# Stores of sixteen heads, V loads behind Q and K: a change to the transfer order of tree attention

## The chip, the cores and the metric

The kernel runs on one core of one Trainium2 chip. The metric is the device time of one execution in microseconds; a time of the kernel is the median of several runs. The 16 transfer (DMA) engines of the core move all data between memory and SBUF. GpSimd (POOL), SyncE (SP) and ScalarE (ACT) issue transfers; loads that turn float32 into bf16 go through GpSimd's queue.

## The reference, cut to what matters

```python
# Q, K, V: (8, 12, 512, 64) float32; 96 heads of 512 x 64
mask = np.zeros((seq, seq))          # node i sees itself and its ancestors in a binary tree
for i in range(seq):
    mask[i, i] = 1
    parent = i
    while parent > 0:
        parent = (parent - 1) // 2
        mask[i, parent] = 1
scores = np.einsum('bhqd,bhkd->bhqk', Q, K) * scale + (1 - mask) * (-1e9)
weights = softmax(scores)            # over the keys
out = np.einsum('bhqk,bhkd->bhqd', weights, V)
```

## The kernel before, in words

Row 4p+t of a head lies on partition p, slot t. A step handles a pair of heads, so there are 48 steps. In step i TensorE makes the scores of pair i (L458, L466, L491, L501), the product with V of pair i - 1 (L551), and in turn the transposes of K (odd steps, L401) or Q (even steps, L433) for two pairs some steps ahead: from step 9 on, step i transposes K of pairs i + 3 and i + 4 in odd steps, Q of pairs i + 2 and i + 3 in even steps. Pairs interlace from pair 8 on, two pairs for four heads, so K and Q of heads 72 to 75 are needed in steps 33 and 34. ScalarE takes the exponentials (L472, L476, L507). VectorE takes reciprocal and product that normalise a pair and write the output tile (L581, L583, in float32), moves transposes out of PSUM (L412 to L420, L441) and makes part of the V copies.

The product with V writes one PSUM tile, `ob`, of which there is one copy; the product of the next pair waits until VectorE has normalised the pair before.

V comes in six tiles of sixteen heads (`vst`, three buffers), each in three transfers: the upper 64 rows, and the even and the odd of the others. It is then copied ("spread") into the layout of the mask, into `vt` (two buffers of three tiles). From tile 4 on, VectorE makes copy "M" of tile o + 1 in two halves of eight heads, at the end of steps 8o and 8o + 2, and copy "Y" at the end of steps 8o + 4 and 8o + 6 (`STEADY_VECTOR`, L695). "M" reads all 128 partitions, so it needs all three transfers of the tile. GpSimd makes the rest: four "top" copies, "X", "Z0" and "Z1" (`spread_top`, `spread_pool`). Copy M of tile 5 (heads 80 to 95) is due in steps 32 and 34, the product with its first heads in step 41.

GpSimd works off a list written out by hand (`pool_program`, L606), in order: loads of K and Q of up to eight heads (1 MB of memory each for eight heads), V in three parts (1, 0.5 and 0.5 MB), its copies, and stores (1 MB for eight heads). `pool(i)` hands out the list as far as `ready` allows; that fixes only the program's order, since the chip's engines wait by semaphores. In the built program a transfer of GpSimd waits besides for the landing of its transfer eight places earlier. Up to head 63 the list is explicit; from head 64 on a loop writes it (L628 to L642): K and Q of eight heads, V parts 32 heads ahead, copies, and a store of eight heads as soon as the heads loaded are `BEHIND` = 56 ahead of it.

Output tiles hold eight heads (`VO`, `NOUT` = 11 buffers). Heads 76 to 79 are stored by SyncE, in four transfers of 64, 27, 25 and 12 rows (`store_apart`, after step 41). Heads 88 to 95 are stored by SyncE and ScalarE two or one at a time as they are ready.

The mask enters the scores through a matrix of codes (L186): 40 rows, loaded by SyncE and copied by ScalarE to partitions 64 and up (L209).

Of the kernel before, what the change touches and what calls it, by code (L numbers as in the profile page):

```python
# [9 lines left out]

CODE = 2048.0
CODE_ROWS = 40
NOUT = 11
BEHIND = 56

# [44 lines left out]
def _nodes(u0, units=UNITS, parity=False):  # L62
    return np.concatenate([4 * _rows(kind, parity) + t for kind, t in units[u0:u0 + 4]])


def _path(n):

    return [1.0 if c == "1" else -1.0 for c in bin(n + 1)[3:]]


def _mask_codes():

    k1 = np.zeros((64, 128), np.float32)
    q1 = np.zeros((64, 4, 128), np.float32)
    k2 = np.zeros((64, 128), np.float32)
    q2 = np.zeros((64, 4, 128), np.float32)  # L80
    k1w = np.zeros((64, 128), np.float32)
    k2w = np.zeros((64, 128), np.float32)

    def key(codes, row, bits, col, node):
        path = _path(node)
        assert len(path) <= bits
        codes[row:row + len(path), col] = np.array(path) * CODE
        codes[row + bits, col] = -len(path) * CODE

    def query(codes, row, bits, col, node):  # L90
        path = _path(node)[:bits]
        codes[(slice(row, row + len(path)),) + col] = path
        codes[(row + bits,) + col] = 1.0

    for c, node in enumerate(_nodes(TOP)):
        key(k1, 0, 7, c, node)
    for c, node in enumerate(_nodes(TOP, WUNITS)):
        key(k1w, 0, 7, c, node)
    for t in range(4):
        for c, node in enumerate(_nodes(TILE2[t])):  # L100
            key(k2, 10 * t, 9, c, node)
        for c, node in enumerate(_nodes(WTILE2[t], WUNITS, True)):
            key(k2w, 10 * t, 9, c, node)
        for p in range(128):
            node = 4 * p + t
            query(q1, 0, 7, (PLACE[t], p), node)
            if p >= 32:
                query(q2, 10 * (SELF[t] if p < 64 else t), 9, (PLACE[t], p), node)
    return np.concatenate([k1, q1.reshape(64, -1), k2, q2.reshape(64, -1), k1w, k2w], axis=1)
# [10 lines left out]
def kernel(  # L120
# [7 lines left out]
    nc = tc.nc  # L128
    B, H, S, D = Q.shape
    P = nc.NUM_PARTITIONS  # L130
    assert S == 512 and D == 64 and P == 128 and (B * H) % 4 == 0
    scale = float(1.0 / np.sqrt(D))
    NH = B * H
    NQ = NH // 4
    NP = 2 * NQ
    WIDE = 8
    KB, VB, VO = 8, 16, 8
    assert NH % VB == 0

    fp32 = mybir.dt.float32  # L140
# [12 lines left out]

    perm_dram = nc.inline_tensor(_eye_twice().astype(ml_dtypes.bfloat16), name="tree_eye")
    code_dram = nc.inline_tensor(
        _mask_codes()[0:CODE_ROWS].astype(ml_dtypes.bfloat16), name="tree_codes"
    )

    ctx.enter_context(tc.manual_schedule())
# [6 lines left out]
    small = ctx.enter_context(tc.tile_pool(name="small", bufs=4))  # L166
    opool = ctx.enter_context(tc.tile_pool(name="opool", bufs=NOUT))
    psS = ctx.enter_context(tc.tile_pool(name="psS", bufs=1, space=bass.MemoryType.PSUM))
# [4 lines left out]
    codes = consts.tile([P, 1536], bf16)  # L173
# [4 lines left out]
    def first_load(eng, name, src):  # L178
        eng.dma_start(
            out=first[name][:, :, :, :].rearrange("p h t d -> p h (t d)"), in_=src[:, 0:2, :]  # L180
        )
# [1 line left out]
    first_load(nc.sync, "K", Kr)  # L183
    nc.scalar.dma_start(out=ptile[:, :], in_=perm_dram.ap())
    first_load(nc.scalar, "Q", Qr)
    nc.sync.dma_start(out=codes[0:CODE_ROWS, :], in_=code_dram.ap())  # L186
    eye = ptile[:, 0:256]

    def eye_blocks(first, x, y):
# [74 lines left out]
    def head(i, a):  # L264

        return 2 * i + a if i < WIDE else 4 * (i // 2) + i % 2 + 2 * a
# [178 lines left out]
    def turn(name, i):  # L445
        heads = [head(i + b, a) for b in range(2 if i >= WIDE else 1) for a in range(2)]
        assert all((name, h) in issued for h in heads), (name, i)
        {"kst": (narrow_k, wide_k), "qst": (narrow_q, wide_q)}[name][i >= WIDE](i)
        return i + (2 if i >= WIDE else 1)
# [140 lines left out]
    def store(eng, h0, n, step=1, p0=0, p1=P):  # L590
        g, f = divmod(h0, VO)
        return eng.dma_start(  # L592
            out=Or[p0:p1, h0:h0 + step * (n - 1) + 1:step, :],
            in_=ofs[g][p0:p1, f:f + step * (n - 1) + 1:step, :, :].rearrange(
                "p h t d -> p h (t d)"
            ),
        )

    APART, APART_AT, APART_ROWS = 76, 41, (0, 64, 91, 116, P)

    def store_apart():

        for p0, p1 in zip(APART_ROWS, APART_ROWS[1:]):
            store(nc.sync, APART, 4, 1, p0, p1)

    def pool_program():  # L606

        ops = [
            (load_k, 2, 2), (load_q, 2, 2), (load_v, 0, 4), (load_v, 4, 4),
            (load_k, 4, 2), (load_k, 6, 2), (load_q, 4, 2), (load_k, 8, 4),  # L610
            (load_q, 6, 2), (load_q, 8, 4), (load_v, 8, 8), (load_k, 12, 4),
            (load_q, 12, 4), (load_k, 16, 4), (load_rows, 1, "upper"),
            (load_q, 16, 4), (load_rows, 1, "even"), (load_k, 20, 4), (load_rows, 1, "odd"),
            (load_q, 20, 4), (load_k, 24, 8), (load_q, 24, 4), (load_rows, 2, "upper"),
            (load_q, 28, 4), (load_k, 32, 4), (load_rows, 2, "even", "odd"),
            (load_q, 32, 8), (load_k, 36, 4), (load_rows, 3, "upper"),
            (spread_pool, (1, "Z0", 8, 16), (1, "Z1", 8, 16)),
            (load_k, 40, 8), (load_q, 40, 8), (load_rows, 3, "even", "odd"),
            (spread_top, 2, 0, 16), (spread_pool, (2, "Z0", 0, 16), (2, "Z1", 0, 16)),
            (load_q, 48, 4), (spread_pool, (2, "X", 0, 8)),  # L620
            (load_k, 48, 8), (spread_pool, (2, "X", 8, 16)),
            (load_q, 52, 4), (load_rows, 4, "upper"), (spread_top, 3, 0, 16),
            (load_k, 56, 8), (load_q, 56, 8), (load_rows, 4, "even", "odd"),
            (spread_pool, (3, "X", 0, 8), (3, "Z0", 0, 16), (3, "Z1", 0, 16), (3, "X", 8, 16)),
            (load_rows, 5, "upper"), (store, nc.gpsimd, 0, VO),
        ]
        loaded, stored = 88, 1
        for h in range(64, NH, KB):  # L628
            top = [(spread_top, h // VB + 0)] if h % VB == 8 and 4 <= h // VB + 0 < NH // VB else []
            ops += [(load_k, h, KB)] + top + [(load_q, h, KB)]  # L630
            while loaded < min(h + 32, NH):
                names = ("even", "odd") if loaded % VB else ("upper",)
                ops.append((load_rows, loaded // VB) + names)
                loaded += KB
            if top:
                o = h // VB
                ops.append((spread_pool, (o, "X", 0, 16), (o, "Z0", 0, 16), (o, "Z1", 0, 16)))
            while VO * stored + VO + BEHIND <= h + KB:
                ops.append((store, nc.gpsimd, VO * stored, VO))
                stored += 1  # L640
        for g in range(stored, NH // VO - 1):
            ops.append((store, nc.gpsimd, VO * g, APART - VO * g if g == APART // VO else VO))  # L642
        return ops

    def ready(op, i):
# [62 lines left out]
    def pool(i):  # L708
        while program and ready(program[0], i):
            op = program.pop(0)  # L710
            op[0](*op[1:])
# [18 lines left out]
    for i in range(NP + 1):  # L730
        steps = FIRST[i] if i < len(FIRST) else "SVK" if i % 2 else "SVQ"
        for step in steps:
            if step == "S" and i < NP:
                scores1(i)
                scores2(i)
            if step == "V" and i >= 1:
                values(i - 1)
                norm(i - 1)
                valued = True
            if step == "K" and kdone < NP:  # L740
                kdone = turn("kst", kdone)
            if step == "Q" and qdone < NP:
                qdone = turn("qst", qdone)
            if step == "W":
                nc.scalar.copy(
                    out=codes[64:64 + CODE_ROWS, 1280:1536], in_=codes[0:CODE_ROWS, 1280:1536]
                )
            if step == "X":
                spin("s1" if valued else "ob", 2)
            if step == "D":  # L750
                spread_by(nc.vector.tensor_copy, BY_VECTOR, STEADY_VECTOR, i)
            if step == "A":
                spread_by(nc.scalar.copy, BY_SCALAR, {}, i)
        if "D" not in steps:
            spread_by(nc.vector.tensor_copy, BY_VECTOR, STEADY_VECTOR, i)
        if "A" not in steps:
            spread_by(nc.scalar.copy, BY_SCALAR, {}, i)
        pool(i)
        if i == APART_AT:
            store_apart()  # L760
        if i >= NP - 3 and i < NP:
            store(nc.sync, head(i - 1, 0), 2, 2)
    assert not program
# [32 lines left out]
```

## Time and profile before

| | |
|---|---|
| median of 3 runs | 135.01 us (134.32 to 135.81) |
| profiled execution, its own time | 134.27 us |
| span of the profiled execution | 132.4 us, clock 0.97 |
| PE busy | 113.4 us (86%) |
| VectorE busy | 100.1 us (76%) |
| ScalarE busy | 94.4 us (71%) |
| GpSimd busy | 72.9 us (55%) |
| memory read, written | 37.94 MB, 12.58 MB |

The span runs from the first to the last instruction; the execution's own time is 1.87 us longer. The page cuts the span into 40 slices of 3.31 us and gives busy shares in tenths. Its chain of waits goes back from the last instruction to whatever released it. A row of the timeline gives start, duration, engine, line and operation, output and input, and in brackets how long the engine was idle before it and what ended that. PE is TensorE, DVE is VectorE, ACT is ScalarE, POOL is GpSimd, SP is SyncE. `kst`, `qst` and `vst` are the loaded K, Q and V; `of` is the output tile; `kq` holds transposed K or Q; `e` the exponentials; `s` and `ob` are PSUM tiles.

### The profile page before, as it was taken

To read this page: it belongs to the slowest core of one execution; us is meant where nothing else is said; L and a number is where in the kernel's file an instruction comes from. 1 tells how busy PE (TensorE), PEld (TensorE's weight loads), DVE (VectorE), ACT (ScalarE), POOL (GpSimd) and SP (SyncE) were. 2 spreads that over 40 slices of the span, in tenths; PEclk is the share of its full clock that TensorE was granted. 3 is DMA by queue.
4 is the path that set the end of the run, shared out by engine and by line. 5 is a ranking of instruction groups with operands and counts; after the bars stand their busy time and mean duration, and the time that the engine had idled before them with its cause. 6 is when DMAs were issued, how large, how long until landed. Compare 5 with 4: busy or idle time off the path is not lost.

```text
span 132.4 us, 5523 instructions
## 1 busy us (share of the span) xinstructions
PE 113.4 (86%) x2414; PEld 79.0 (60%) x2417; DVE 100.1 (76%) x249; ACT 94.4 (71%) x153; POOL 72.9 (55%) x100
## 2 busy tenths in 40 slices
PE   6886979999999899899989299999999997989800
PEld 2343755766676677676766276767666774756500
DVE  3539779889999999987965668899978896674620
ACT  4369577988888788778768455889796975969600
POOL 6999625454375999987732799437289600002000
PEclk9999999999999999999999958999999999999985
DMA  3999999999999999999999999999999999999992
GB/s 109 237 184 193 199 196 201 202 202 205 199 202 201 203 203 207 200 210 197 205 204 197 298 273 202 266 300 226 341 214 330 244 279 399 401 399 401 395 351 72
DMA packets 32244, 32.26 MB, mean 244 GB/s; under 512 B 1204, under 2 KB 29492, under 8 KB 32220
## 3 DMA queue, kind: packets, MB, share of 16 engines
q0 software_dynamic: 29824, 29.63, 114.7%
q1 hardware_dynamic: 1836, 1.83, 4.0%
q10 hardware_dynamic: 560, 0.46, 1.1%
q8 instruction: 19, 0.31, 0.9%
q14 instruction: 5, 0.04, 0.1%
HBM read 37.94 MB, written 12.58 MB: 382 GB/s over the span
## 4 chain that ended last, share of the span: by engine, by line
DMA 57%; PE 26%; POOL 5%; issue 4%; ACT 2%; DVE 1%; ACTq 0%; POOLq 0%
DMA vst<-in_V_dram 38%; DMA qst<-in_Q_dram 13%; PE ob L551 8%; DMA kst<-in_K_dram 7%; PE s L458 4%; PE s L466 3%; PE qtp L433 3%; PE ktp L401 2%; PE s L491 2%; PE s L501 2%; POOL vt L336 2%; POOL kst L251 1%; PE s L551 1%; ACT e L472 1%; ACT e L507 1%
## 5 line engine op out<-in xcount | busy, mean ns | idle before, releaser
L476 ACT ACTIVATE e<-s 128x1024 bf16<-128x1024 f32 x40 | 40.9, 1023 | 21.5 <-PE s L466 20.8
L551 PE MATMUL ob<-vt,e 128*128 128x65 bf16 (+1 forms) x940 | 38.0, 198 | 5.2 <-DVE of L583 3.8
L551 PEld LDWEIGHTS <-e 128*128 128x128 bf16 (+1 forms) x960 | 30.6, 103 | 13.7 <-DVE of L583 4.0
L507 ACT ACTIVATE e<-s 128x384 bf16<-128x384 f32 x80 | 34.7, 491 | 0.0
L583 DVE TENSOR_TENSOR of<-ob,rec 128x512 f32<-128x512 f32 x47 | 32.5, 691 | 1.6
L336 POOL COPY vt<-vst 32x512 int32<-32x512 int32 (+1 forms) x32 | 24.1, 754 | 7.2 <-DVE vt L336 3.9
L336 DVE COPY vt<-vst 64x1024 bf16<-64x1024 bf16 (+6 forms) x42 | 17.6, 420 | 5.7 <-DMA vst<-in_V_dram 5.1
L458 PE MATMUL s<-codes 40*128 40x512 bf16 x96 | 19.6, 395 | 1.2 <-issue 0.4
L581 DVE RECIPROCAL rec<-ob 128x8 f32<-128x8 f32 x47 | 9.7, 205 | 13.3 <-PE ob L551 12.7
L466 PE MATMUL s<-kq 64*128 64x512 bf16 x96 | 18.8, 382 | 0.0
L592 POOL DMA_DIRECT2D out_dram<-of x11 | 9.8, 895 | 15.5 <-DVE of L583 13.4
L280 POOL DMA_DIRECT2D vst<-in_V_dram x15 | 10.8, 723 | 12.7 <-DMA vst<-in_V_dram 7.0
L501 PEld LDWEIGHTS <-kq 64*128 64x128 bf16 x320 | 12.6, 95 | 4.7 <-issue 0.4
L501 PE MATMUL s<-kq 64*128 64x160 bf16 (+1 forms) x320 | 15.1, 210 | 0.0
L491 PE MATMUL s<-codes 40*128 40x384 bf16 x80 | 14.1, 339 | 0.1
L401 PE MATMUL ktp<-ptile,kst 128*64 128x128 bf16 x320 | 12.9, 224 | 1.2 <-issue 0.9
L441 DVE COPY kq<-qtp 128x1024 bf16<-128x1024 bf16 x20 | 13.6, 682 | 0.2 <-PE qtp L433 0.2
L433 PE MATMUL qtp<-ptile,qst 128*64 128x128 bf16 x320 | 12.7, 219 | 0.8 <-issue 0.7
L251 POOL DMA_DIRECT2D qst<-in_Q_dram x13 | 9.6, 738 | 5.1 <-DMA kst<-in_K_dram 1.7
L251 POOL DMA_DIRECT2D kst<-in_K_dram x12 | 9.1, 756 | 5.6 <-PE s L466 1.6
L491 PEld LDWEIGHTS <-codes 40*128 40x128 bf16 x80 | 6.4, 95 | 8.8 <-issue 1.1
L472 ACT ACTIVATE e<-s 128x1024 bf16<-128x1024 f32 x8 | 8.2, 1022 | 4.9 <-PE s L466 4.8
(42 smaller groups left out, 120.2 us busy)
## 6 DMA issues: line engine op xcount, KB each, us to landing
out_dram<-of POOLq DMA_DIRECT2D x10, 1024.0 KB, 16.3
kst<-in_K_dram POOLq DMA_DIRECT2D x8, 512.0 KB, 15.3
qst<-in_Q_dram POOLq DMA_DIRECT2D x7, 512.0 KB, 16.8
vst<-in_V_dram POOLq DMA_DIRECT2D x12, 256.0 KB, 14.1
vst<-in_V_dram POOLq DMA_DIRECT2D x6, 512.0 KB, 13.4
qst<-in_Q_dram POOLq DMA_DIRECT2D x8, 256.0 KB, 11.7
kst<-in_K_dram POOLq DMA_DIRECT2D x6, 256.0 KB, 11.7
out_dram<-of SPq DMA_DIRECT2D x4, 256.0 KB, 7.3
```

Of the source, the lines that this page charges most:

```text
L251: return nc.gpsimd.dma_start(out=kept[b][:, h0 % KB:h0 % KB + n, :, :].rearrange("p (g x) t d -> p g (x t d)", x=2), in_=wide[:, h0 // 2:( ...
L336: return copy(out=dst, in_=src)
L401: nc.tensor.transpose(out=columns(kp[64 * a:64 * a + 64, :], mixed, (256, 2), (leaves - mixed, 2), (1, 32)), in_=st[:, 2 * i % KB // 2 + a ...
L433: nc.tensor.transpose(out=halves[64 * a:64 * a + 64, :, c:c + 64], in_=st[:, 2 * i % KB // 2 + a, 4 * u + t, :], identity=ptile[:, 0:128],)
L458: nc.tensor.matmul(out=sp[:, a, :], lhsT=(k1code if i < WIDE else k1wide)[64 * a:64 * a + CODE_ROWS, :], rhs=(q1code[64 * a:64 * a + CODE_ ...
L466: nc.tensor.matmul(out=sp[:, a, :], lhsT=keys(i, a, TOP), rhs=qTs[i][64 * a:64 * a + 64, :, :].rearrange("p t c -> p (t c)"), start=False, ...
L476: ) if i < WIDE else nc.scalar.activation(
L491: nc.tensor.matmul(out=flat[:, a, :, :].rearrange("p u (t c) -> p u t c", t=4)[:, :, :, 16:64], lhsT=k2wide[64 * a:64 * a + CODE_ROWS, :], ...
L501: nc.tensor.matmul(out=flat[:, a, :, lo:hi], lhsT=keys(i, a, WTILE2[t]), rhs=qT[64 * a:64 * a + 64, :, lo:hi], start=False, stop=t == 1, s ...
L507: nc.scalar.activation(out=e2s[i % NE][:, a, :, 32:128].rearrange("p t (r u) -> p t r u", u=2), in_=flat[:, a, :, :].rearrange("p u (t r) ...
L551: nc.tensor.matmul(out=ob[lo:hi, a, 65 * t:65 * t + 65], lhsT=e[:, a, PLACE[t], lo:hi], rhs=vt[vtile[tile_v][0]][:, head(i, a) % VB, vtile ...
L583: nc.vector.tensor_tensor(out=ofs[g][:, first:last + 1:step, :, :], in0=o4[:, a:a + n, :, 0:D], in1=rec[:, a:a + n, :, :].to_broadcast([P, ...
```

## The change

Output tiles hold sixteen heads and there are six of them. GpSimd's list is written out to its end. From head 64 on its order is: K64, Q64, store 0 to 15; K72, the top copies of V tile 4, Q72, Z0 and Z1; V tile 5 upper, X of tile 4, V tile 5 even and odd; K80, Q80, store 16 to 23; K88, Q88; stores 24 to 31 and 32 to 47; top, Z0 and Z1 of tile 5; store 48 to 63; X of tile 5; stores 64 to 71, 72 to 79, 80 to 87. `store_apart` goes, and with it the four transfers of SyncE. Q of heads 48 to 55 is one load and not two. The codes are loaded with 48 rows, of which 40 are used as before. The tables of VectorE's and ScalarE's copies stay.

```diff
-NOUT = 11
-BEHIND = 56
+NOUT = 6
+LOAD_ROWS = 48
...
-    KB, VB, VO = 8, 16, 8
+    KB, VB, VO = 8, 16, 16
...
-        _mask_codes()[0:CODE_ROWS].astype(ml_dtypes.bfloat16), name="tree_codes"
+        _mask_codes()[0:LOAD_ROWS].astype(ml_dtypes.bfloat16), name="tree_codes"
...
-    nc.sync.dma_start(out=codes[0:CODE_ROWS, :], in_=code_dram.ap())
+    nc.sync.dma_start(out=codes[0:LOAD_ROWS, :], in_=code_dram.ap())
...
-    APART, APART_AT, APART_ROWS = 76, 41, (0, 64, 91, 116, P)
-
-    def store_apart():
-
-        for p0, p1 in zip(APART_ROWS, APART_ROWS[1:]):
-            store(nc.sync, APART, 4, 1, p0, p1)
...
-            (load_q, 48, 4), (spread_pool, (2, "X", 0, 8)),
+            (load_q, 48, 8), (spread_pool, (2, "X", 0, 8)),
             (load_k, 48, 8), (spread_pool, (2, "X", 8, 16)),
-            (load_q, 52, 4), (load_rows, 4, "upper"), (spread_top, 3, 0, 16),
+            (load_rows, 4, "upper"), (spread_top, 3, 0, 16),
             (load_k, 56, 8), (load_q, 56, 8), (load_rows, 4, "even", "odd"),
             (spread_pool, (3, "X", 0, 8), (3, "Z0", 0, 16), (3, "Z1", 0, 16), (3, "X", 8, 16)),
-            (load_rows, 5, "upper"), (store, nc.gpsimd, 0, VO),
+            (load_k, 64, 8), (load_q, 64, 8), (store, nc.gpsimd, 0, 16),
+            (load_k, 72, 8), (spread_top, 4), (load_q, 72, 8),
+            (spread_pool, (4, "Z0", 0, 16), (4, "Z1", 0, 16)),
+            (load_rows, 5, "upper"), (spread_pool, (4, "X", 0, 16)),
+            (load_rows, 5, "even", "odd"), (load_k, 80, 8), (load_q, 80, 8),
+            (store, nc.gpsimd, 16, 8), (load_k, 88, 8), (load_q, 88, 8),
+            (store, nc.gpsimd, 24, 8), (store, nc.gpsimd, 32, 16),
+            (spread_top, 5), (spread_pool, (5, "Z0", 0, 16), (5, "Z1", 0, 16)),
+            (store, nc.gpsimd, 48, 16), (spread_pool, (5, "X", 0, 16)),
+            (store, nc.gpsimd, 64, 8), (store, nc.gpsimd, 72, 8), (store, nc.gpsimd, 80, 8),
         ]
-        loaded, stored = 88, 1
-        for h in range(64, NH, KB):
-            top = [(spread_top, h // VB + 0)] if h % VB == 8 and 4 <= h // VB + 0 < NH // VB else []
-            ops += [(load_k, h, KB)] + top + [(load_q, h, KB)]
...
-        for g in range(stored, NH // VO - 1):
-            ops.append((store, nc.gpsimd, VO * g, APART - VO * g if g == APART // VO else VO))
...
-        if i == APART_AT:
-            store_apart()
```

More of the change, by code (lines that the diff above doesn't have):

```diff
@@ L619, in pool_program @@
             (spread_top, 2, 0, 16), (spread_pool, (2, "Z0", 0, 16), (2, "Z1", 0, 16)),
-            (load_q, 48, 4), (spread_pool, (2, "X", 0, 8)),
+            (load_q, 48, 8), (spread_pool, (2, "X", 0, 8)),
             (load_k, 48, 8), (spread_pool, (2, "X", 8, 16)),
-            (load_q, 52, 4), (load_rows, 4, "upper"), (spread_top, 3, 0, 16),
+            (load_rows, 4, "upper"), (spread_top, 3, 0, 16),
             (load_k, 56, 8), (load_q, 56, 8), (load_rows, 4, "even", "odd"),
             (spread_pool, (3, "X", 0, 8), (3, "Z0", 0, 16), (3, "Z1", 0, 16), (3, "X", 8, 16)),
-            (load_rows, 5, "upper"), (store, nc.gpsimd, 0, VO),
-        ]
-        loaded, stored = 88, 1
-        for h in range(64, NH, KB):
-            top = [(spread_top, h // VB + 0)] if h % VB == 8 and 4 <= h // VB + 0 < NH // VB else []
-            ops += [(load_k, h, KB)] + top + [(load_q, h, KB)]
[L631 to L640, printed above, removed]
-        for g in range(stored, NH // VO - 1):
-            ops.append((store, nc.gpsimd, VO * g, APART - VO * g if g == APART // VO else VO))
+            (load_k, 64, 8), (load_q, 64, 8), (store, nc.gpsimd, 0, 16),
[8 more added lines that the diff above has]
+            (store, nc.gpsimd, 64, 8), (store, nc.gpsimd, 72, 8), (store, nc.gpsimd, 80, 8),
+        ]
         return ops
```

## The prediction

> **What bounds the kernel now.** I read the page's slices first, then stages by window, then the chain of waits, then the rows of the engines that the chain names. The slices say that the transfer engines are never without work:
>
> ```profile
> PEclk9999999999999999999999958999999999999985
> DMA  3999999999999999999999999999999999999992
> GB/s 109 237 184 193 199 196 201 202 202 205 199 202 201 203 203 207 200 210 197 205 204 197 298 273 202 266 300 226 341 214 330 244 279 399 401 399 401 395 351 72
> HBM read 37.94 MB, written 12.58 MB: 382 GB/s over the span
> ```
>
> The DMA row is full from the second slice to the last but one. GB/s counts bytes on the SBUF side, where a load arrives as bf16; a load at 200 reads 400 from memory, and a pure store stage moves 400. So every stage moves about 400 GB/s of memory traffic, and the 37.94 + 12.58 = 50.52 MB of the last line alone take some 126 us of the 132.4. No order of the transfers changes that sum; an order can only change who waits for what, and how the end looks. The end, by windows (us, busy of the five engines, clock, DMA share, GB/s):
>
> ```profile
> 109.00:122.00 13.00, 11.51 (x260) 8.17 (x256) 8.37 (x19) 9.97 (x17) 0.90 (x1) 1.00 1.03 401
> 126.00:129.00 3.00, 0.00 (x0) 0.00 (x0) 0.48 (x2) 0.00 (x0) 0.00 (x0) 0.82 0.97 352
> 129.00:132.40 3.40, 0.00 (x0) 0.00 (x0) 0.00 (x0) 0.00 (x0) 0.00 (x0) 0.50 0.23 77
> 131.00:132.40 1.40, 0.00 (x0) 0.00 (x0) 0.00 (x0) 0.00 (x0) 0.00 (x0) 0.50 0.00 0
> ```
>
> Arithmetic ends at about 126.5 and 352 x 3 + 77 x 3.4 = 1318 KB are still to go; they are gone by 131. So two things end together: transfers, and the chain of arithmetic whose last store is part of that remainder. The chain of waits (start, us, what) tells what paces the arithmetic:
>
> ```profile
> 9.85 9.59 DMA kst<-in_K_dram
> 57.62 16.22 DMA vst<-in_V_dram
> 77.68 16.82 DMA qst<-in_Q_dram
> 94.54 0.64 PE qtp L433 x16
> ```
>
> The last link to a load is Q of heads 72 to 79, landed at 77.68 + 16.82 = 94.50; from there PE works without a load's wait to the end. The link before is the last part of V tile 4 (heads 64 to 79), landed at 57.62 + 16.22 = 73.84. GpSimd's rows between those two (all loads, and most stores, go through its one queue):
>
> ```profile
> 62.47 0.81 POOL L280 DMA_DIRECT2D vst<-in_V_dram  x1
> 63.27 0.90 POOL L592 DMA_DIRECT2D out_dram<-of  x1
> 64.17 0.76 POOL L251 DMA_DIRECT2D kst<-in_K_dram  x1
> 65.80 0.89 POOL L251 DMA_DIRECT2D qst<-in_Q_dram  x1 [0.87 <-PE s L501]
> 68.89 0.66 POOL L280 DMA_DIRECT2D vst<-in_V_dram  x1 [2.21 <-DMA kst<-in_K_dram]
> 71.40 0.65 POOL L280 DMA_DIRECT2D vst<-in_V_dram  x1 [1.84 <-DMA qst<-in_Q_dram]
> 72.74 0.90 POOL L592 DMA_DIRECT2D out_dram<-of  x1 [0.69 <-DMA vst<-in_V_dram]
> 74.38 0.76 POOL L251 DMA_DIRECT2D kst<-in_K_dram  x1 [0.74 <-DMA vst<-in_V_dram]
> 77.68 0.74 POOL L251 DMA_DIRECT2D qst<-in_Q_dram  x1
> ```
>
> With 1 MB for 8 heads of anything in float32 (V's upper rows 1, even and odd 0.5 each), these nine carry 8 MB. They landed in 94.50 - 73.84 = 20.66 us: 2.58 us for each MB, in the order of issue, with 16 us of queue ahead of each.
>
> **The change, part by part.**
>
> *Loads from head 64 on (the term that decides).* Before, V tile 5 (heads 80 to 95) ends 5 MB after V tile 4 (V upper 1, store 1, K64 1, Q64 1, even and odd 1): 73.84 + 5 x 2.58 = 86.7. After, ahead of its end lie K64 1, Q64 1, the store of sixteen heads 2, K72 1, Q72 1, V upper 1, even and odd 1: 8 MB, so it lands at 94.5, where Q72 landed before. Q72 in its turn comes at 73.84 + 6 x 2.58 = 89.3. K80, Q80, K88 and Q88 each come 1 MB, 2.6 us, earlier than before, so none of them can newly be late. But the table of VectorE's copies is not changed: step 32 still ends with the copy "M" of V tile 5, which needs all three parts. VectorE takes its work in order, and the next normalisation stands behind the copy. What that costs is seen once already, at the copy for V tile 4 (first row), and the second row is the same copy for tile 5:
>
> ```profile
> 74.03 0.43 DVE L336 COPY vt<-vst 128x1024 bf16<-128x1024 bf16 x1 [2.60 <-DMA vst<-in_V_dram]
> 91.69 0.53 DVE L336 COPY vt<-vst 128x1024 bf16<-128x1024 bf16 x1
> 126.09 0.42 DVE L583 TENSOR_TENSOR of<-s,rec 128x256 f32<-128x256 f32 x1
> ```
>
> PE's rows around the two places:
>
> ```profile
> 75.35 0.79 PE L551 MATMUL ob<-vt,e 128*128 128x65 bf16 x20 [2.48 <-DVE of L583]
> 75.97 0.61 PE L433 MATMUL qtp<-ptile,qst 128*64 128x128 bf16 x16
> 76.52 0.46 PE L458 MATMUL s<-codes 40*128 40x512 bf16 x2
> 80.02 0.44 PE L458 MATMUL s<-codes 40*128 40x512 bf16 x2
> 82.15 0.40 PE L458 MATMUL s<-codes 40*128 40x512 bf16 x2
> 93.60 0.79 PE L551 MATMUL ob<-vt,e 128*128 128x65 bf16 x20
> 109.35 0.79 PE L551 MATMUL ob<-vt,e 128*128 128x65 bf16 x20
> ```
>
> Landing 73.84, copy 0.19 later, product with V (L551, which has one PSUM tile and so waits for the normalisation) 1.32 after that, Q's transposes 0.62 later. The same steps from 94.5 give copy 94.7, product 96.0 instead of 93.60, transposes 96.6 instead of 94.54: the arithmetic is **2.1 us later** from there on. The copy at 91.69 had 5.0 us to spare; it is 7.8 us later, so the stall is 2.8 us, less what the wait for Q72 took before. Bounds: if PE already runs late, less; it can't be below 0.3 us gained (the wait for Q72 alone), nor above 2.8.
>
> *The clock after the stall.* The stall at 75.35 had a second price:
>
> ```profile
> 73.30:76.70 3.40, 1.35 (x38) 1.14 (x40) 2.60 (x8) 1.08 (x3) 2.54 (x5) 1.00 1.23 329
> 76.70:80.10 3.40, 3.40 (x52) 2.44 (x50) 2.14 (x5) 1.79 (x3) 3.26 (x5) 0.50 1.19 238
> ```
>
> After a stretch with PE busy 1.35 of 3.40 us, the granted clock was 0.50 for the next 3.4 us; the step from 76.52 to 80.02 took 3.50 us where the next took 2.13. Cost 1.37 us, which before was lost in the later wait for Q72 and after is not, for nothing is left to wait for. The new stall leaves PE idle for 96.0 - 93.6 = 2.4 us, as long as the old 2.48, so I take the price again: between 0 and 1.4, I take **1.3 us**, with a chance of about two in three. [...]
>
> *The end.* The last store's price:
>
> ```profile
> 119.35 0.90 POOL L592 DMA_DIRECT2D out_dram<-of  x1 [13.38 <-DVE of L583]
> 126.55 0.35 ACTq L592 DMA_DIRECT2D out_dram<-of  x1
> out_dram<-of ACTq DMA_DIRECT2D x1, 128.0 KB, 4.8
> ptile<-tree_eye ACTq DMA_DIRECT2D x1, 64.0 KB, 2.5
> ```
>
> Issued at 126.55, landed 4.8 later beside a full queue (131.35), and 1.05 to the end of the span. After, arithmetic ends 2.1 or 3.4 us later, when the 1318 KB have shrunk by 390 KB/us to little more than the last heads' own data. So its landing is nearer to the 64 KB at the start, 2.5 us, than to 4.8; I take **2.6**, 2.2 us less. The queue does not run dry before: GpSimd's last store (119.35) moves to about 122.8, when some 2.5 MB are left of which it and the last eight heads are 2.1.
>
> *Stores of sixteen heads; 72 to 79 in one.* The bytes are the same. GpSimd's issue time is 0.90 us per 8 heads either way. GpSimd now has the 2 MB stores ahead of the last V copies:
>
> ```profile
> 90.01 2.68 POOL L336 COPY vt<-vst 32x512 int32<-32x512 int32 x4 [2.01 <-PE ob L551]
> 96.43 3.20 POOL L336 COPY vt<-vst 32x1024 int32<-32x1024 int32 x3 [3.05 <-DVE vt L336]
> ```
>
> In the built program each of its DMAs waits for the landing of the one eight places earlier, so the store of 32 to 47 goes out when V's even rows land (93.2). Then come 1.8 + 2.68 + 3.20 + 1.8 = 9.5 us: done at 103. They are first needed by the product of head 80, at 109.35 before and later after: cost 0, six us of cover. If the cover went, its excess would be on the path one to one. SyncE drops four DMAs and nothing stands behind them but its own last stores.
>
> *Q48 in one load, codes of 48 rows.* K48 lands 0.5 MB, 1.3 us, later; PE waits 2.48 us at 75.35 for V anyway, which covers it: 0. For the codes ScalarE waited 1.4 us:
>
> ```profile
> ACT codes L209 <- DMA codes<-tree_codes: 1.4, 1, 1.4
> ```
>
> At most that is to be gained or lost; but the chain's next link is K landed at 9.85 + 9.59 = 19.44, behind the full queue, which does not move: 0.
>
> *Sum.* +2.1 +1.3 -2.2 = **+1.2 us** on a span of 132.4. The profiled execution took 134.27, 0.74 below the median of 135.01; from the median 136.2.
>
> **The rivals.**
>
> *B, stall without half clock.* +2.1 - 2.2: **134.9**. For it: the bigger part of the stall may fall across two clock stretches. Against: the fence above.
>
> *C, faster: an evener end.* The 1318 KB at 392 take 3.4 us, which would end them at 129.4, not near 131: some of the 16 engines finish up to 1.5 us after the rest. The four SyncE stores of 64, 27, 25 and 12 rows, which go, may be the cause. If they are and the V copy does not hold PE (its landing under 91.7), the end moves by -1.5: **133.5**. It decides only when arithmetic ends by 126.6. Against: the FIFO arithmetic. [...] No row of the views here shows single engines.
>
> *D, slower still.* Stall 2.8, clock 1.4, last landing not shortened by more than 1.1 because the stores of the last heads crowd one another: +3.1, **138.1**. It decides if the last landing takes over 3.7.
>
> **How the numbers follow.** The forecast (A) 0.48: 136.2, own range 135.4 to 136.9. B 0.24, C 0.14, D 0.14. About 1% (133.7 to 136.4) is what a measurement of this kernel can tell from no change. Faster 0.13 (C), same 0.50 (B and most of A), slower 0.37 (D and the rest of A). The range of 133.8 to 137.6 leaves out the far half of C and D.
>
> **What would show it.** Right: a VectorE wait of some 2.8 us for V just before a 128x1024 copy near 94.6; PE idle 2.4 us before the product at 96; a 0.50 clock stretch after it; Q72 no longer in the chain; the last ScalarE store issued 128.5 to 130 and landing in under 3 us. Wrong: the copy of tile 5 runs without a wait, the end of arithmetic stays at 126.5, or the DMA row shows gaps before 126.

## The result, and the profile after

The changed kernel takes 135.85 us (median of 18 runs) against 135.06 for the kernel before (18 runs): ratio **1.0083**, 95% interval 1.0054 to 1.0112. The two medians alone give less, 0.79 us or a ratio of 1.0058. The changed kernel is slower by 0.6 to 0.8%, inside the bound of 1% that the prediction set; the interval leaves out 1. The profiled execution took 135.49 with a span of 133.7; before it was 134.27 and 132.4. One profile of the experiments (uneven stores back, V late) caught one of that kernel's long executions and is not read below.

The page's slices of the changed kernel:

```profile
PEclk9999999999999999999999856999999999999995
DMA  3999999999999999999999999999999999999971
GB/s 105 231 194 194 200 197 201 200 203 206 198 202 202 202 203 205 201 209 198 206 202 203 218 386 325 209 199 199 209 327 241 282 406 396 404 399 369 380 282 67
HBM read 37.96 MB, written 12.58 MB: 378 GB/s over the span
```

The transfers are as dense as before until 120 us; what is new is a dent in the slices near the end (369, 380, 282) and a longer stretch of half clock. The page's chain of waits, by line:

```profile
DMA 36%; PE 28%; DVE 17%; POOL 7%; issue 5%; ACT 3%; ACTq 0%; DVEq 0%; POOLq 0%
DMA vst<-in_V_dram 28%; PE ob L551 10%; DMA kst<-in_K_dram 7%; DVE of L583 6%; DVE vt L336 5%; PE s L458 4%; POOL vt L336 4%; PE s L466 3%; PE ktp L401 3%; PE qtp L433 2%; PE s L501 2%; PE s L491 2%; ACT e L507 2%; DVE rec L581 2%; DVE kq L441 1%
```

Q is gone from it (it was the last load there before), and V with VectorE's copies is left at its end. VectorE's rows: the first M copies of V tiles 4 and 5, and the last normalising product.

```profile
74.27 1.12 DVE L336 COPY vt<-vst 128x1024 bf16<-128x1024 bf16 x1 [2.49 <-DMA vst<-in_V_dram]
...
95.75 0.78 DVE L336 COPY vt<-vst 128x1024 bf16<-128x1024 bf16 x1 [1.78 <-DMA vst<-in_V_dram]
...
129.34 0.42 DVE L583 TENSOR_TENSOR of<-s,rec 128x256 f32<-128x256 f32 x1
```

PE's rows behind them:

```profile
76.28 1.20 PE L551 MATMUL ob<-vt,e 128*128 128x65 bf16 x20 [3.06 <-DVE of L583]
77.30 1.04 PE L433 MATMUL qtp<-ptile,qst 128*64 128x128 bf16 x16
...
97.43 0.79 PE L551 MATMUL ob<-vt,e 128*128 128x65 bf16 x20 [1.12 <-DVE of L583]
98.06 0.61 PE L433 MATMUL qtp<-ptile,qst 128*64 128x128 bf16 x16
```

The copy for tile 5, which had 5 us to spare, now waits for V, and Q's transposes come at 98.06 where they came at 94.54. But only part of that is the new wait. PE was late already: the product at 75.35 before stands at 76.28, and the clock stays low for twice as long (windows: us, busy of the engines, granted clock, DMA share, GB/s):

```profile
72.50:75.90 3.40, 0.72 (x14) 0.37 (x10) 1.60 (x3) 1.91 (x4) 3.29 (x4) 1.00 1.25 204
75.90:79.30 3.40, 3.02 (x42) 2.16 (x44) 3.05 (x8) 0.00 (x0) 0.00 (x0) 0.50 1.13 337
79.30:82.70 3.40, 3.40 (x52) 2.34 (x48) 1.60 (x5) 1.79 (x3) 3.22 (x5) 0.50 1.05 370
```

The product at 76.28 is 0.93 us late because the copy of tile 4 started 0.24 us later (74.27 against 74.03) and took 0.69 longer. Beside it run GpSimd's copies Z0 and Z1 of V tile 4, which the new order puts ahead of the V loads:

```profile
72.98 2.12 POOL L336 COPY vt<-vst 32x1024 int32<-32x1024 int32 x2
```

They run until 75.10, and the M copy beside them takes 1.12 and not 0.43 us. The end of the span, first by windows, then the last ScalarE store and its landing:

```profile
126.00:129.00 3.00, 2.47 (x52) 1.75 (x49) 1.79 (x5) 1.79 (x3) 0.00 (x0) 1.00 0.84 314
129.00:132.40 3.40, 0.00 (x0) 0.00 (x0) 0.73 (x3) 0.00 (x0) 0.00 (x0) 0.72 0.53 182
131.00:132.40 1.40, 0.00 (x0) 0.00 (x0) 0.00 (x0) 0.00 (x0) 0.00 (x0) 0.50 0.13 45
```

```profile
129.79 0.35 ACTq L592 DMA_DIRECT2D out_dram<-of  x1
out_dram<-of ACTq DMA_DIRECT2D x1, 128.0 KB, 2.6
```

Arithmetic ends 3.25 us later (129.34 against 126.09 in start of the last product), the last store lands 2.6 and not 4.8 us after its issue, and the span is 1.3 longer: 3.25 - 2.2 = 1.05, and 0.26 more between the landing and the end of the span.

### The profile page after: what moved, and what is told of

It is laid out like the page before. It is cut to its first block, busy times and chain, and to the rows that moved or that the text cites. A ratio compares the mean times of both kernels' runs of the same rounds, so it can differ in the third digit from the quotient of the medians.

```text
span 133.7 us, 5514 instructions
## 1 busy us (share of the span) xinstructions
PE 114.5 (86%) x2414; PEld 79.9 (60%) x2417; DVE 101.1 (76%) x249; ACT 94.4 (71%) x153; POOL 70.6 (53%) x96
## 4 chain that ended last, share of the span: by engine, by line
DMA 36%; PE 28%; DVE 17%; POOL 7%; issue 5%; ACT 3%; ACTq 0%; DVEq 0%; POOLq 0%
DMA vst<-in_V_dram 28%; PE ob L551 10%; DMA kst<-in_K_dram 7%; DVE of L583 6%; DVE vt L336 5%; PE s L458 4%; POOL vt L336 4%; PE s L466 3%; PE ktp L401 3%; PE qtp L433 2%; PE s L501 2%; PE s L491 2%; ACT e L507 2%; DVE rec L581 2%; DVE kq L441 1%
## 5 line engine op out<-in xcount | busy, mean ns | idle before, releaser
L551 PE MATMUL ob<-vt,e 128*128 128x65 bf16 (+1 forms) x940 | 38.3, 199 | 7.2 <-DVE of L583 5.1
L551 PEld LDWEIGHTS <-e 128*128 128x128 bf16 (+1 forms) x960 | 31.0, 104 | 15.9 <-DVE of L583 5.7
L336 DVE COPY vt<-vst 64x1024 bf16<-64x1024 bf16 (+6 forms) x42 | 19.8, 472 | 8.0 <-DMA vst<-in_V_dram 6.3
L592 POOL DMA_DIRECT2D out_dram<-of x8 | 8.1, 1014 | 22.0 <-DVE of L583 18.1
L251 POOL DMA_DIRECT2D qst<-in_Q_dram x12 | 8.8, 736 | 5.6 <-PE ktp L401 2.7
```

The source lines that it names most:

```text
L251: return nc.gpsimd.dma_start(out=kept[b][:, h0 % KB:h0 % KB + n, :, :].rearrange("p (g x) t d -> p g (x t d)", x=2), in_=wide[:, h0 // 2:( ...
L336: return copy(out=dst, in_=src)
L551: nc.tensor.matmul(out=ob[lo:hi, a, 65 * t:65 * t + 65], lhsT=e[:, a, PLACE[t], lo:hi], rhs=vt[vtile[tile_v][0]][:, head(i, a) % VB, vtile ...
```

## The experiments

The theories, by their letters. **S**: the late V tile 5 holds VectorE's copy and with it all arithmetic (the prediction). **E**: the end of the transfers got worse. **U** (the prediction's rival C): the four uneven SyncE stores made the engines end apart, so that leaving them out helps. **B**, its opposite: they relieved engines that run late. **Q**: it was the second queue that helped, not the rows. **Z**: Z0 and Z1 beside M start PE late, a second cause in a row with S. **W**: transfers of 2 MB delay what stands behind them. **M**, formed after the first eight runs: the end is the later of two, the transfers, and arithmetic plus some 2.6 us. Each kernel was timed in five rounds against the kernel before.

### V tile 5 early again, in the changed kernel

```diff
-            (load_k, 64, 8), (load_q, 64, 8), (store, nc.gpsimd, 0, 16),
+            (load_rows, 5, "upper"), (load_k, 64, 8), (load_q, 64, 8),
+            (load_rows, 5, "even", "odd"), (store, nc.gpsimd, 0, 16),
...
-            (load_rows, 5, "upper"), (spread_pool, (4, "X", 0, 16)),
-            (load_rows, 5, "even", "odd"), (load_k, 80, 8), (load_q, 80, 8),
+            (spread_pool, (4, "X", 0, 16)),
+            (load_k, 80, 8), (load_q, 80, 8),
```

> The changed kernel with only the three loads of V tile 5 put back where the kernel before has them: upper before K64, even and odd after Q64. Theory S (the late V holds VectorE's copy, and so the arithmetic): the copy of tile 5 runs without a wait, arithmetic ends at 126 to 127 us and not at 129.8, the span falls from 133.7 to about 132.2, ratio to the kernel before 0.990 to 1.002. Rival E (the end of the transfers got worse: 2 MB stores, SyncE's four stores gone): the wait goes, but the ratio stays at 1.006 to 1.010.

Ratio 1.0014 (0.9984 to 1.0045): most of the loss is gone, and of all the runs that undo one part of the change this is the only one whose interval lies wholly below that of the whole change. VectorE's copy of tile 5 and ScalarE's last store:

```profile
91.76 0.41 DVE L336 COPY vt<-vst 128x1024 bf16<-128x1024 bf16 x1
```

```profile
126.48 0.35 ACTq L592 DMA_DIRECT2D out_dram<-of  x1
out_dram<-of ACTq DMA_DIRECT2D x1, 128.0 KB, 5.3
```

The copy does not wait, and arithmetic ends as before. S holds as to the place, with one reservation: with the V loads ahead of them in GpSimd's list, Z0 and Z1 of tile 4 start only at 77.03, so they no longer run beside the first M copy either, and this run undoes both. The span fell less than expected, to 133.1: the landing takes 5.3 us again, half a microsecond more than before.

### V tile 5 late alone, in the kernel before

```diff
-            (load_rows, 5, "upper"), (store, nc.gpsimd, 0, VO),
+            (store, nc.gpsimd, 0, VO),
...
-            while loaded < min(h + 32, NH):
...
+            if h == 72:
+                ops += [(load_rows, 5, "upper"), (load_rows, 5, "even", "odd")]
```

> The kernel before with only the loads of V tile 5 moved behind Q72; stores of eight heads, SyncE's four stores and the 40 rows of codes stay. Theory S: VectorE waits 1.5 to 3 us for V before the first copy of tile 5, arithmetic ends 2 to 3.5 us later than 126.5, ratio 1.004 to 1.012. Rival E: the wait is there, but the ratio is 1.00 within 0.003, since the end is as before.

Ratio 1.0021 (0.9987 to 1.0054): the delay is there, the cost hardly.

```profile
95.11 0.43 DVE L336 COPY vt<-vst 128x1024 bf16<-128x1024 bf16 x1 [1.89 <-POOL vt L336]
```

```profile
128.95 0.35 ACTq L592 DMA_DIRECT2D out_dram<-of  x1
out_dram<-of ACTq DMA_DIRECT2D x1, 128.0 KB, 2.7
```

The last store is issued 2.4 us later than before (126.55) and lands at 131.65, 0.3 later: 2.1 of 2.4 us are given back at the end. (The row names GpSimd as releaser, whose top copies of the same tile end just then; they need V's upper rows alone, the M copy all of V. Which of the two came last, the row does not settle.) S by itself, without the end, does not account for this time.

### The uneven stores left out, in the kernel before

```diff
-            ops.append((store, nc.gpsimd, VO * g, APART - VO * g if g == APART // VO else VO))
+            ops.append((store, nc.gpsimd, VO * g, VO))
...
-        if i == APART_AT:
-            store_apart()
```

> The kernel before with heads 72 to 79 stored by GpSimd in one transfer and SyncE's four stores of 64, 27, 25 and 12 rows left out. [...] Theory S alone: 1.000 within 0.003. Rival E (the four stores helped): 1.003 to 1.008, with a longer tail after the last store is issued.

Ratio 1.0038 (1.0008 to 1.0068), so slower: U has the wrong sign. The last microseconds of the transfers, in the kernel before and then in this one:

```profile
130.00:131.00 1.00, 0.00 (x0) 0.00 (x0) 0.00 (x0) 0.00 (x0) 0.00 (x0) 0.50 0.22 76
131.00:132.00 1.00, 0.00 (x0) 0.00 (x0) 0.00 (x0) 0.00 (x0) 0.00 (x0) 0.50 0.00 0
```

```profile
130.00:131.00 1.00, 0.00 (x0) 0.00 (x0) 0.00 (x0) 0.00 (x0) 0.00 (x0) 0.50 0.32 112
131.00:132.00 1.00, 0.00 (x0) 0.00 (x0) 0.00 (x0) 0.00 (x0) 0.00 (x0) 0.50 0.14 47
```

```profile
126.55 0.35 ACTq L592 DMA_DIRECT2D out_dram<-of  x1
out_dram<-of ACTq DMA_DIRECT2D x1, 128.0 KB, 5.5
```

The store is issued at 126.55 in both, and lands 5.5 in place of 4.8 us later. Without the uneven rows the last store lands 0.7 us later, with arithmetic unchanged.

### The same heads by SyncE in even rows

```diff
-    APART, APART_AT, APART_ROWS = 76, 41, (0, 64, 91, 116, P)
+    APART, APART_AT, APART_ROWS = 76, 41, (0, P)
```

> The kernel before with heads 76 to 79 stored by SyncE in one transfer of 128 rows in place of four of 64, 27, 25 and 12. Theory B (the uneven rows take work from engines that are late): the last GpSimd store lands over a spread of some 5 us as without the SyncE stores, ratio 1.002 to 1.006. Rival Q (what helped is a second queue beside GpSimd's): ratio 0.998 to 1.001.

Ratio 1.0019 (0.9989 to 1.0048), which does not tell B from Q. The transfers of the profiled execution end as late as without the SyncE stores:

```profile
131.00:132.00 1.00, 0.00 (x0) 0.00 (x0) 0.00 (x0) 0.00 (x0) 0.00 (x0) 0.50 0.14 48
```

That speaks for B, though arithmetic ended 0.8 us later in this execution. Two more readings of the record say the same. The signals that tell of the landing of GpSimd's last store come over 5.0 us, as without SyncE's stores (5.2) and not as in the kernel before (4.15). And the median span of the executions is 133.55, again as without SyncE's stores (133.55), where the kernel before has 132.80. The times of whole executions leave it open, and one reason is on record too: outside the span lay 2.9 to 3.6 us in 26 of the 116 executions of the kernel before that were timed beside the experiments, and never over 2.2 in the 114 of the kernels without the uneven rows. So the rows shorten the span, and some executions lose more than that outside it; why is open.

### The uneven rows twice

```diff
+        if i == 37:
+            store_apart(68)
         if i == APART_AT:
-            store_apart()
+            store_apart(APART)
```

GpSimd then stores only heads 64 to 67 of 64 to 71.

> The kernel before with a second set of four uneven SyncE stores: heads 68 to 71 after step 37, besides 76 to 79 after step 41. Theory B (some engines are late through the whole run, and the uneven rows relieve them): the last GpSimd store lands over a spread of 3 to 3.5 us and not 4.2, last landing 130.6 to 131.2, ratio 0.994 to 0.999. If one set already evens the engines out, a second makes others late: 1.002 to 1.008.

Ratio 1.0027 (0.9996 to 1.0059): no gain, so more of the same does not help. The last store lands at 127.83 + 3.9 = 131.7, against 131.35 before, and GpSimd's last store lands over 4.9 us where 3 to 3.5 were expected.

### VectorE's copies of tile 5 later, in the changed kernel

```diff
+    LATE_VECTOR = {4: [("M", 0, 8)], 5: [("M", 8, 16)], 6: [("Y", 0, 8)], 7: [("Y", 8, 16)]}
```

used for tile 5 alone.

> The changed kernel with the four VectorE copies of V tile 5 put into steps 36 to 39 in place of 32, 34, 36 and 38; the transfers are as changed. Theory S: no wait for V tile 5, PE does not idle near 96, and Q72 is there early, so arithmetic ends at 125.5 to 127, ratio 0.990 to 1.002. Rival E: ratio 1.006 to 1.010. If the copies come too late for the product of head 80 in step 41, PE waits there up to 1 us.

Ratio 1.0043 (1.0020 to 1.0067), between what S and E gave. PE no longer stalls near 96, but arithmetic still ends late, at 128.7. What is left is the first stall:

```profile
74.49 1.17 DVE L336 COPY vt<-vst 128x1024 bf16<-128x1024 bf16 x1 [2.44 <-DMA vst<-in_V_dram]
```

```profile
76.55 0.79 PE L551 MATMUL ob<-vt,e 128*128 128x65 bf16 x20 [3.05 <-DVE of L583]
```

This is where Z was formed: the wait for tile 5 had hidden a start that was late already.

### Both late, and Z0 and Z1 behind X

```diff
-            (spread_pool, (4, "Z0", 0, 16), (4, "Z1", 0, 16)),
-            (load_rows, 5, "upper"), (spread_pool, (4, "X", 0, 16)),
+            (load_rows, 5, "upper"),
+            (spread_pool, (4, "X", 0, 16), (4, "Z0", 0, 16), (4, "Z1", 0, 16)),
```

on top of the last edit.

> The changed kernel with VectorE's copies of V tile 5 in steps 36 to 39, as before, and besides GpSimd's copies Z0 and Z1 of V tile 4 behind its X, so that they no longer run while VectorE makes the first M copy of tile 4. Theory Z (two stalls in a row: Z beside M lengthens that copy from 0.43 to 1.1 us and starts PE late from 76 on, and the wait for V tile 5 takes whatever of it is left): the M copy at 74 takes 0.4 to 0.5, the product after it starts at 75.3 to 75.7, arithmetic ends at 126 to 127.5, ratio 0.999 to 1.003. Theory S alone (only the wait for tile 5): no change against the run with the late VectorE copies alone, 1.004.

Ratio 1.0027 (0.9997 to 1.0058).

```profile
73.90 0.43 DVE L336 COPY vt<-vst 128x1024 bf16<-128x1024 bf16 x1 [1.12 <-DMA vst<-in_V_dram]
```

```profile
75.22 0.79 PE L551 MATMUL ob<-vt,e 128*128 128x65 bf16 x20 [1.01 <-DVE of L583]
```

```profile
127.14 0.35 ACTq L592 DMA_DIRECT2D out_dram<-of  x1
out_dram<-of ACTq DMA_DIRECT2D x1, 128.0 KB, 5.4
```

The copy takes 0.43 again and arithmetic ends 1.6 us sooner than in the run before, 0.6 of it because the copy could start sooner: Z is shown as a mechanism, in one execution. The last landing, 132.5, is no sooner than that of the run before (128.71 + 3.4 = 132.1). In the kernels without the uneven rows the last landing lies at 132.0 to 132.5 wherever arithmetic ends, but for the run with V early (131.8). This run and the one without uneven stores are what M rests on.

### Stores of eight heads, and codes of 40 rows, in the changed kernel

The first cuts each store of sixteen heads into two of eight; the second sets `LOAD_ROWS = 40`.

> The changed kernel with GpSimd's three stores of sixteen heads each cut into two of eight, at the same places. Theory S and Z: the bytes ahead of V tile 5 are the same, so the wait and the ratio stay, 1.005 to 1.011. Rival W (transfers of 2 MB make the loads behind them land late): V tile 5 lands a microsecond sooner, at 94.5, ratio 1.002 to 1.005.

> The changed kernel with the codes loaded with 40 rows as before. [...] If the codes don't matter: 1.006 to 1.010.

Ratios 1.0047 (1.0004 to 1.0090) and 1.0040 (1.0008 to 1.0072). The first lies in W's range (1.002 to 1.005), the second below the range for codes that don't matter (1.006 to 1.010), but the one interval reaches beyond W's range, the other into that of the codes, and both overlap with that of the whole change. So neither edit is shown to matter, nor to be without effect. V tile 5 landed just before the copies at 95.19 and 94.92 (95.75 in the changed kernel), where W expected 94.5. With 40 rows of codes the copy of tile 4 started at 74.34 (74.27 in the changed kernel), so by then the loads were no sooner.

### The uneven stores back in the changed kernel, with V late and with V early

In both, SyncE stores heads 76 to 79 as before the change; the second has V tile 5 early besides.

> The changed kernel with one part undone: heads 76 to 79 again stored by SyncE in four transfers of 64, 27, 25 and 12 rows after step 41. The late V tile 5 stays. Theory M (the end is the later of two: the transfers, which without the uneven rows land last at 132.3, and arithmetic plus 2.6 us): the transfers could end near 131.3 again, but arithmetic ends at 128.5 to 129.8, so the last landing is 131.3 to 132.4 and the ratio 1.002 to 1.007, with runs near 137 still among them. Rival B alone (only the uneven rows count): ratio 0.998 to 1.002.

> The changed kernel with both undone: V tile 5 loaded early and the four uneven SyncE stores back. What is left of the change are tiles and stores of sixteen heads, the order of K, Q and stores, Q48 in one load and codes of 48 rows. Theory M: both ends are as before, last landing 131.0 to 131.6, ratio 0.996 to 1.001. If something else of the change costs time: 1.002 or more.

Ratios 1.0054 (1.0016 to 1.0092) and 1.0005 (0.9961 to 1.0048). The rows alone do not mend the change; with V early, what is left of it (sixteen heads, the order of K and Q, the codes) is neither shown to gain nor to lose. In the second run's profiled execution 136.19 - 133.0 = 3.2 us lay outside the span, as in two more of its twelve, which widens its interval. Its arithmetic ended 2.75 us late (last product at 128.84) although V came early and the copy of tile 5 did not wait; the delay builds up over many steps, and its cause is open.

### The two parts alone, in the kernel before

V tile 5 late and heads 72 to 79 by GpSimd, all else as before.

> The kernel before with two parts of the change alone: V tile 5 behind Q72, and heads 72 to 79 stored by GpSimd in one transfer. Tiles and stores of eight heads, the other order, Q48 in two loads and 40 rows of codes stay. Theory M (the end is the later of the transfers, at about 132.3 without the uneven rows, and of arithmetic plus 2.6 us): arithmetic ends at 128.5 to 129.5, last landing 132.0 to 132.6, ratio 1.004 to 1.008, the whole change within its interval. Rival Z (the rest of the change, above all Z0 and Z1 beside M, is needed for the whole): 1.001 to 1.004.

Ratio 1.0051 (1.0013 to 1.0090), in the range of M (1.004 to 1.008) and not in that of Z (1.001 to 1.004), though the interval reaches into it; the whole change's 1.0083 lies in the interval. The last store, and the clock around the stall at the second place:

```profile
130.00 0.35 ACTq L592 DMA_DIRECT2D out_dram<-of  x1
out_dram<-of ACTq DMA_DIRECT2D x1, 128.0 KB, 2.4
```

```profile
93.90:97.30 3.40, 1.30 (x40) 1.01 (x35) 2.09 (x6) 1.79 (x3) 1.94 (x3) 1.00 1.14 305
97.30:100.70 3.40, 3.40 (x52) 2.25 (x48) 1.88 (x5) 1.59 (x3) 1.30 (x2) 0.50 1.23 234
```

Here the prediction's sequence is complete: late V, idle PE, half clock from 97.3, arithmetic to 130, landing in 2.4.

## Why the prediction was right, and where it was not

*Loads from head 64 on, +2.1.* Right in place and kind, too small in the changed kernel. V tile 5 landed just before 95.75, not at 94.5, about 1.2 us later than the count of 8 MB gave, and its copy took 0.78 us and not 0.43. So Q's transposes came 3.5 us later (98.06 against 94.54) and not 2.1. In the other runs that keep V late with the copy in its place, that copy started between 94.9 and 95.2. Why the 8 MB took longer in the changed kernel is not shown.

The wait for V also hides what was lost before it. VectorE's normalising product ahead of the copy and the next one behind it, in the changed kernel and then in the run with 40 rows of codes:

```profile
92.69 0.69 DVE L583 TENSOR_TENSOR of<-ob,rec 128x512 f32<-128x512 f32 x1
96.69 0.69 DVE L583 TENSOR_TENSOR of<-ob,rec 128x512 f32<-128x512 f32 x1
```

```profile
90.59 0.69 DVE L583 TENSOR_TENSOR of<-ob,rec 128x512 f32<-128x512 f32 x1
95.64 0.69 DVE L583 TENSOR_TENSOR of<-ob,rec 128x512 f32<-128x512 f32 x1
```

In the kernel before they stand at 90.49 and 92.58. With V tile 5 late alone they are at 91.93 and 95.69, with stores of eight heads at 92.40 and 95.76, with the two parts alone at 91.12 and 95.75. So the product behind the copy stands 3.1 to 3.2 us later than before in four runs and 4.1 in the changed kernel, whether the arithmetic ahead of it was late by 2.2 us or by 0.1. The first stall, with GpSimd's Z0 and Z1 beside the copy and the longer half clock, does not add to the wait for V; it counts where that wait is taken away, as in the run with VectorE's copies later. The prediction put GpSimd's work at nothing because its copies were early enough, and did not ask what they ran beside. What is left of the delay at the end of arithmetic differs from run to run: 3.25 us in the changed kernel, 2.4 with V late alone, 1.9 with 40 rows of codes, 3.45 with the two parts alone.

*The clock, +1.3.* In the changed kernel the term did not come where it was put. In its profiled execution the half clock came after the first stall and for two stretches, and none after the second, where PE idled only 1.12 us because it came late itself. With the two parts alone it came after both, and behind the second the delay of the normalising products grew from 2.9 to 4.0 us, 1.1 us for the predicted 1.3. So 3.25 us of late arithmetic against the predicted 2.1 + 1.3 is luck: a later landing and a slower copy stand in the place of the clock. Of the idle times in the last section the longest is 3.31 us, and 2.08 was enough once.

*The last landing, -2.2.* Right: 2.6 measured for 2.6. It is also why the late V alone costs 0.2% and not 1.8% (2.4 us).

*SyncE's four stores, cost 0, and rival C a gain.* Wrong; this is the step that failed. The prediction reckoned from the bytes left that some engines finish up to 1.5 us after the rest, and took the uneven stores for the possible cause, where they were a partial remedy: without them the time is 1.0038 of before (1.0008 to 1.0068), and the last store of an otherwise unchanged kernel lands 0.7 us later. With them the last landings of the profiled executions are 131.3 to 131.9; without them 132.0 to 132.5, with arithmetic ending anywhere from 126.5 to 130; 131.8 only with V early. Since the end is the later of two, late arithmetic costs little until its last store passes the transfers; that it costs all of its delay from there on follows from M and was not measured. In the changed kernel the last store lands at 132.4, where both ends meet.

*The sum.* Predicted 1.2 us, measured 0.8 by the medians (135.85 - 135.06) and 1.1 by the ratio. The total is right in part by luck: the delay of arithmetic has other terms than the forecast, and the forecast leaves out the cost of SyncE's stores, which alone make 0.0038. By single parts in the kernel before: V late 0.0021, no uneven rows 0.0038, both 0.0051. By undoing in the changed kernel: V early leaves 0.0014, uneven rows leave 0.0054, both leave 0.0005. What makes 0.0083 of 0.0051 is not settled. The three runs that undo one other part with V still late (uneven rows back, stores of eight heads, codes of 40 rows) gave 0.0040 to 0.0054, and the medians of the whole change give 0.0058, so part of the difference may be chance. Z beside M is no good candidate while V is late, by the rows above; the stores of sixteen heads and the codes stay possible. Why V early alone recovers nearly all, though the uneven rows are still missing there, is open as well; its transfers ended 0.3 to 0.8 us sooner than those of the other kernels without the rows, in one execution.

*Stores of sixteen heads, cost 0.* GpSimd's V copies were done at 102.7, as predicted (103). Its issue of such a store took 1.2 us, not the 1.8 that the prediction reckoned.

No version is shown to beat the kernel before.

## What to carry to other kernels

With transfers saturated, a load moved back landed later by somewhat more than its bytes over the rate: V tile 5, behind 3 MB more, landed 8.96 us later (95.67 against 86.71) where 2.58 us for each MB gives 7.74. Its first reader is what counts: look for the engine that makes that read, and for what stands behind it there (here VectorE, the product at 96.69 behind the copy at 95.75). A kernel whose transfers and arithmetic end together has two ends; price each alone, and a delay of one only from where it passes the other. A wait for a load can hide what was lost before it (here 0.1 to 2.2 us): ask what is hidden before adding two delays. An odd-looking split of a store may earn its place (here the last store landed 0.7 us later without it): measure it alone before calling it waste.

## What the runs showed of the hardware

- **Half clock after 2.08 us or more of PE idling.** In twelve profiled executions of this study, the product (L551) behind an M copy of tile 4 or 5 that came after PE had idled 2.08 us or more (2.08, 2.09, 2.10, 2.14, 2.31, 2.48, 3.05, 3.06, 3.31) met a clock of 0.50 at its start or within 1.5 us of it in eight of nine cases, for one or two stretches of 3.4 us (76.73 to 80.14 in the kernel before, 75.87 to 82.70 in the changed kernel); after 0.50 to 2.03 us (eight cases) never. The exception is 2.14, in the run with the uneven rows twice.
- **VectorE's copy beside GpSimd's.** The same 128x1024 bf16 copy takes 0.42 to 0.43 us with no copy of GpSimd beside it (74.03 and 95.88 in the kernel before, 79.00 in the changed kernel). It took 1.12 beside GpSimd's second 32x1024 copy in the changed kernel, and 1.15 and 1.17 at the same place with stores of eight heads and with VectorE's copies later. Beside GpSimd's 32x512 copies it took 0.53 (91.69 in the kernel before), 0.78 and 1.08 (95.75 and 99.72 in the changed kernel). GpSimd's pair of 32x1024 copies ends at 75.10, the copy that began at 74.27 ends 0.29 later; what holds it up meanwhile is not shown.
- **The last store, of 128 KB, lands 2.4 to 2.7 us after its issue when that comes at 128.95 or later, and 4.8 to 5.5 when it comes at 126.5 to 127.4**; in three executions between the two (127.8 to 128.7) it took 3.4 to 3.9. In the changed kernel some 0.38 MB were still moved after the issue (98 GB/s over 3.91 us), in the kernel before 1.09 MB (187 GB/s over 5.85 us).
- **Uneven rows went with an earlier end of the transfers in the kernel before.** Its last store lands at 131.3, without them at 132.05, issued at 126.55 in both. GpSimd's last store of 1 MB landed over 4.15 us with SyncE's stores of 64, 27, 25 and 12 rows ahead of it, and over 5.0 with one of 128 rows and 5.2 with none. In the changed kernel, which has no uneven rows, it was issued at 122.58 and not 119.35 and landed over 2.6 us.
